# The first shift and scale of a decoder block, moved from VectorE to TensorE, with six projection blocks in step

## The chip, the cores and the metric

The kernel runs on one core of a Trainium2 chip. The metric is the device time of one execution, in microseconds (us). Five engines work side by side, each with its own list of instructions that it takes in order: TensorE (PE; its weight loads are shown apart, as PEld), VectorE (DVE), ScalarE (ACT), GpSimd (POOL) and SyncE (SP), which issues the DMA transfers. They wait for one another through semaphores.

## The reference, cut to what matters

A decoder block for one sequence of 2048 positions and 1024 channels, all in float32. A condition vector `c` gives six vectors of 1024 numbers, two of which, a shift and a scale, go into the first norm:

```python
cond = jax.nn.silu(c)
mod = (cond @ w_ada + b_ada)                 # 1024 x 6144
sh1, sc1, g1, sh2, sc2, g2 = split(mod, 6)
h = rms_norm(x, norm1_g) * (1 + sc1) + sh1
proj = h @ w_in                              # 1024 x 3088
# gated linear attention on 4 heads, dilated attention on 8 heads, one output projection
x = x + g1 * (mixed @ w_out)
# second norm with sh2, sc2; up projection, convolution of width 3, SwiGLU, down projection
x = x + g2 * ffn
```

Nothing of the projection can start before the shift and the scale are there for at least one group of 128 channels, and they need two sixths of `w_ada`, 8 MB.

## The kernel before, in words

The 2048 positions are four chunks of 512. Channels lie on the 128 partitions, so that 1024 channels are eight groups `k` = 0 to 7. A product in float32 is made of three faster ones (`mm3`, L234 to L241): the weight is split into a rounded part `whi` and the rest `wlo`, the activation into `hhi` and `hlo`, and three matmuls add hi by hi, lo by hi and hi by lo. `wslot` (L213) loads a weight block, ScalarE casts it to `whi` (L223), and VectorE or GpSimd subtracts to get `wlo` (L224).

At the start (`run`, L878) x of chunk 0 is loaded, `norm_stats` sums its squares (one matmul with a matrix of 1/1024, L318), and then for each `k` a shift and a scale are made by `ada(b)`, where `b` numbers the 48 groups of 128 columns of `w_ada`, 0 to 7 the shift and 8 to 15 the scale: a transposed weight block of 128 x 1024 is loaded (L275), VectorE multiplies it with `cond`, which lies in all partitions, and sums along the row (L281), then reads the sum out, adds the bias (L282) and, for the scale, makes `G` (L286). In this text such a multiply-and-sum is called a product. With them `norm_mod1` gives `hhi` (L333, ScalarE) and `hlo` (L335, VectorE) of that `k`. Four blocks of the projection (`FIRST`, channel blocks 0 to 3, the q and k of the gated attention) accumulate in four PSUM banks as the `k` come in. The low halves of their weights are all made on GpSimd.

The other 32 products (`b` = 16 to 47, shift, scale and gates of later stages) run beside the projections of all four chunks. They share one buffer (tile `v4`, one of it), so a load can start only when the product before it has read the buffer. The first of these loads, the load of the constants and the loads of x for chunk 1 each wait for a gate (`after`), the product of `k` = 6. A scheduler that works with a cost model at build time sets the final order on every engine, from the order in which the code hands the operations out. In the projection of chunk 0 (`proj`, L339) the four blocks already summed are stored first (`glaqk`), and then come the token-major block `tok(0)` (matmuls of 272 columns, its weight being 128x1088) and the blocks of the dilated attention (`qk`). The same `tok(0)` opens the projection of chunk 1. Later, `L552` copies the first state of the gated attention into `sbd`, after the last of the 32 products.

## Time and profile before

| | |
|---|---|
| median of 3 runs | 2752.87 us (2747.39 to 2753.99) |
| profiled execution, its own time | 2751.32 us |
| its span | 2749.5 us |
| mean granted TensorE clock | 0.984 |
| TensorE busy | 2658.3 us, 97% |
| VectorE busy | 1890.0 us, 69% |
| ScalarE busy | 1275.4 us, 46% |
| GpSimd busy | 515.7 us, 19% |

In the profile's rows the first number is the start in us from the start of the span, the second the duration, then engine, line, operation, output <- inputs and shapes; `xN` counts instructions, and brackets hold idle time before, with what ended it. In a table by windows each engine has its busy time with a count; PEclk is the clock that the throttle granted TensorE, as a share of full speed.

### The profile page before, as it was taken

What the parts mean: (1) busy time and instruction counts of PE and PEld (TensorE: products, weight loads), DVE (VectorE), ACT (ScalarE), POOL (GpSimd) and SP (SyncE); (2) the same over time, 40 slices, a digit from 0 to 9 for tenths busy, and PEclk for the clock granted to TensorE, in tenths of its full rate; (3) what the DMA queues carried; (4) which work ended last, traced back from release to release, by engine and by line L of the source; (5) the groups of instructions that cost most, each with busy time, mean ns of one, the idle gap of its engine ahead of it and who ended that gap; (6) DMA issues with size and microseconds to landing.
All of it is one profiled execution on the core that took longest, in us unless ns stands there. A gap on an engine that the chain in (4) does not pass through costs nothing.

```text
span 2749.5 us, 48364 instructions
## 1 busy us (share of the span) xinstructions
PE 2658.3 (97%) x18920; PEld 2178.2 (79%) x18920; DVE 1890.0 (69%) x3740; ACT 1275.4 (46%) x2607; POOL 515.7 (19%) x324
## 2 busy tenths in 40 slices
PE   5988999999999999999999999999999999999999
PEld 3977898888878777777777777887877778788887
DVE  8778676545578676667987667679676666566655
ACT  3555556564645434453544444345444443343332
POOL 1334322212224111101321101023111000021110
PEclk9998999999999999999999999999999999999999
DMA  7877465445722433346444334553444325332222
GB/s 272 289 257 235 144 200 172 154 156 168 243 84 94 135 121 113 105 141 206 135 124 127 111 121 128 176 167 104 142 129 131 123 90 181 129 100 97 95 100 92
DMA packets 196230, 405.19 MB, mean 147 GB/s; under 512 B 19473, under 2 KB 78626, under 8 KB 194722
## 3 DMA queue, kind: packets, MB, share of 16 engines
q1 hardware_dynamic: 196002, 402.11, 45.0%
q8 instruction: 149, 2.44, 0.4%
q14 instruction: 79, 0.65, 0.1%
HBM read 339.12 MB, written 62.91 MB: 146 GB/s over the span
## 4 chain that ended last, share of the span: by engine, by line
PE 78%; DVE 8%; DMA 6%; ACT 4%; issue 3%; POOL 1%; SPq 0%; ACTq 0%; POOLq 0%; DVEq 0%
PE psg L239 22%; PE psg L241 22%; PE psg L240 22%; DMA wada<-in_w_ada_dram 3%; PE psa L725 3%; PE psa L630 3%; PE psa L751 3%; DMA sq<-in_xT_dram 1%; DVE wada L281 1%; DVE wlo L224 1%; PE psa L500 1%; DVE pt L520 1%; ACT big L640 1%; ACT whi L223 1%; PE psa L650 1%
## 5 line engine op out<-in xcount | busy, mean ns | idle before, releaser
L239 PE MATMUL psg<-hhi,whi 128*128 128x512 f32 x2040 | 813.2, 401 | 19.6 <-ACT hhi L333 9.2
L240 PE MATMUL psg<-hlo,whi 128*128 128x512 f32 x2040 | 808.9, 397 | 5.6 <-DVE hlo L335 4.1
L241 PE MATMUL psg<-hhi,wlo 128*128 128x512 f32 x2040 | 808.5, 398 | 4.9 <-DVE wlo L224 4.8
L223 ACT CAST whi<-wraw 128x1024 fp32r<-128x1024 f32 x391 | 409.0, 1050 | 531.9 <-PE psg L240 375.4
L224 DVE TENSOR_TENSOR wlo<-wraw,whi 128x1024 fp32r<-128x1024 f32 (+1 forms) x300 | 388.3, 1296 | 163.1 <-ACT whi L223 148.7
L224 POOL TENSOR_TENSOR wlo<-wraw,whi 128x1024 fp32r<-128x1024 f32 x91 | 225.6, 2480 | 1433.0 <-ACT whi L223 1231.3
L239 PEld LDWEIGHTS psg<-hhi,whi 128*128 128x128 f32 x2040 | 389.0, 191 | 111.9 <-ACT hhi L333 12.2
L241 PEld LDWEIGHTS psg<-hhi,wlo 128*128 128x128 f32 x2040 | 389.0, 191 | 93.6 <-DVE wlo L224 6.4
L240 PEld LDWEIGHTS psg<-hlo,whi 128*128 128x128 f32 x2040 | 389.3, 191 | 91.5 <-DVE hlo L335 6.3
L239 PE MATMUL psg<-ghi,whi 128*128 128x512 f32 x704 | 277.9, 395 | 0.0
L241 PE MATMUL psg<-ghi,wlo 128*128 128x512 f32 x704 | 275.6, 392 | 1.1 <-DVE wlo L224 1.1
L240 PE MATMUL psg<-glo,whi 128*128 128x512 f32 x704 | 275.9, 392 | 0.0
L870 DVE SCALAR_TENSOR_TENSOR x<-psg,mod,x 128x512 f32<-128x512 f32 x192 | 143.0, 749 | 143.0 <-PE psg L241 138.3
L239 PE MATMUL psg<-whi,hhi 128*128 128x256 f32 (+1 forms) x768 | 220.9, 289 | 3.7 <-ACT hhi L333 1.9
L241 PE MATMUL psg<-whi,hlo 128*128 128x256 f32 (+1 forms) x768 | 220.4, 289 | 3.7 <-DVE hlo L335 3.7
L240 PE MATMUL psg<-wlo,hhi 128*128 128x256 f32 (+1 forms) x768 | 220.0, 287 | 0.4 <-DVE wlo L224 0.4
L826 DVE SCALAR_TENSOR_TENSOR y<-psg,conv_w_sb,y 128x511 f32<-128x511 f32 x176 | 130.6, 743 | 84.4 <-ACT y L825 84.1
L239 PEld LDWEIGHTS psg<-ghi,whi 128*128 128x128 f32 x704 | 132.2, 188 | 30.1 <-issue 2.9
L241 PEld LDWEIGHTS psg<-ghi,wlo 128*128 128x128 f32 x704 | 132.2, 188 | 30.0 <-DVE wlo L224 1.6
L240 PEld LDWEIGHTS psg<-glo,whi 128*128 128x128 f32 x704 | 132.3, 188 | 28.2 <-issue 2.1
L239 PEld LDWEIGHTS psg<-whi,hhi 128*128 128x128 f32 x768 | 147.9, 193 | 7.4 <-issue 2.2
L241 PEld LDWEIGHTS psg<-whi,hlo 128*128 128x128 f32 x768 | 147.9, 193 | 5.4 <-DVE hlo L335 4.4
(195 smaller groups left out, 3746.1 us busy)
## 6 DMA issues: line engine op xcount, KB each, us to landing
wraw<-in_w_up_dram SPq DMA_DIRECT2D x176, 512.0 KB, 3.4
wraw<-in_w_down_dram SPq DMA_DIRECT2D x88, 512.0 KB, 3.4
wraw<-in_w_ch_dram SPq DMA_DIRECT2D x48, 512.0 KB, 4.1
wada<-in_w_ada_dram SPq DMA_DIRECT2D x40, 512.0 KB, 5.0
wraw<-in_w_tok_dram SPq DMA_DIRECT2D x40, 512.0 KB, 4.3
v<-v SPq DMA_DIRECT2D x68, 256.0 KB, 4.2
wraw<-in_w_out_dram SPq DMA_DIRECT2D x32, 512.0 KB, 4.4
sq<-in_xT_dram SPq DMA_DIRECT2D x48, 256.0 KB, 3.9
```

Source lines behind the costliest of these rows:

```text
L223: nc.scalar.copy(hi[:, :n], raw[:, :n])
L224: (nc.gpsimd if pool else nc.vector).tensor_tensor(lo[:, :n], raw[:, :n], hi[:, :n].bitcast(F32), op=ALU.subtract)
L239: nc.tensor.matmul(ps, wh, hh, start=first and k == 0, stop=False, skip_group_check=shared)
L240: nc.tensor.matmul(ps, wh, hl, start=False, stop=False, skip_group_check=shared)
L241: nc.tensor.matmul(ps, wl, hh, start=False, stop=k == n - 1, skip_group_check=shared)
L281: self.last = nc.vector.tensor_tensor_reduce(raw, raw, self.cond[:, i * n:(i + 1) * n], 0.5, m if i else 0.0, ALU.mult, ALU.add, m)
L500: nc.tensor.matmul(sp[j:j + w, n * w:(n + 1) * w], kh[R, k0:k0 + w], qh[R, q0:q0 + w], start=True, stop=True)
L630: nc.tensor.matmul(ps[hh][:, e * 256 + z:(e + 1) * 256], q[H[hh], (i + e) * P:(i + e + 1) * P], key(H[hh], i + e, z), start=True, stop=Tru ...
L725: nc.tensor.transpose(ps[:n, i * P:(i + 1) * P], part(S[hh], i), self.C("id"))
L751: nc.tensor.matmul(out, lhsT, rhs, start=first[hh], stop=False, skip_group_check=True)
L826: nc.vector.scalar_tensor_tensor(y[:, 1:], ps[:, :T - 1], self.cw[:, 1, b:b + 1], y[:, 1:], op0=ALU.mult, op1=ALU.add)
L870: nc.vector.scalar_tensor_tensor(x1, ps, self.mod[:, 40 + cb:41 + cb], x1, op0=ALU.mult, op1=ALU.add)
```

## The change

The first 2048 columns of `w_ada` are laid out anew on the host, as `w_ada1`: four groups `u` of two `k` each, a group being four loads of 512 KB. `ada_first(u)` multiplies them on TensorE. The stationary side is `cond` with the 128 channels of group `k` on the partitions, the same number repeated in 32 columns (`crep`), the moving side 512 columns of `w_ada1`; the eight matmuls of a group go in turn to four bands of 32 columns of the array, each with 32 partitions of one PSUM bank. ScalarE copies the bank to SBUF, four small matmuls with a column of 1/64 (`sel`) sum the bands and turn the result onto the partitions, and VectorE adds the bias for two `k` of shift and of scale in one instruction (L310) and makes `G1` (L311). The 16 products of the first stage and their bias adds are gone from VectorE; the other 32 stay.

`FIRST` has six blocks where it had four, the two more being the first two of the dilated attention, in two banks of the other PSUM pool; after each group the matmuls of all six blocks for its two `k` are handed out. The low halves of blocks 1, 3 and 5 are made on GpSimd, those of 0, 2 and 4 on VectorE. The gate is now the bias add of group `u` = 2. In chunk 0, `qk(0)` and `qk(1)`, which are now only stored, come ahead of `tok(0)`.

```diff
-GATE = 6
-FIRST = (0, 1, 2, 3)
+FIRST = (0, 1, 2, 3, 4, 5)
...
+        self.sel = self.const.tile([P, 1], F32, name="sel")
+        nc.vector.memset(self.sel, 1.0 / 64)
+        tc_ = self.const.tile([P, KD], F32, name="tcol")
+        nc.scalar.activation(tc_, cc, AF.Tanh, scale=0.5)
+        self.crep = self.const.tile([P, KD, 32], F32, name="crep")
+        rep = lambda t: t[:, :, None].to_broadcast([P, KD, 32])
+        nc.vector.scalar_tensor_tensor(self.crep, rep(tc_), 1.0, rep(cc), op0=ALU.add, op1=ALU.mult)
...
+    def ada_first(self, u):
+        nc = self.nc
+        ps = self.pa()
+        raws = []
+        for i in range(4):
+            raw = self.at.tile([P, 1024], F32, name="wada", tag="big", bufs=4)
+            nc.sync.dma_start(raw, self.A["w_ada1"][u, i])
+            raws.append(raw)
+        for k in range(KD):
+            j = k % 4
+            nc.tensor.matmul(ps[32 * j:32 * j + 32], self.crep[:, k], raws[k // 2][:, k % 2 * T:(k % 2 + 1) * T], start=k < 4, stop=k >= 4, skip_group_check=True)
+        t = self.tmp.tile([P, T], F32, name="sq", bufs=3)
+        nc.scalar.copy(t, ps)
+        pm = self.pa()
+        for i in range(4):
+            nc.tensor.matmul(pm[:, i:i + 1], t[:, i * P:(i + 1) * P], self.sel, start=True, stop=True, skip_group_check=True)
+        v = lambda t: t.rearrange("p (a k) -> p a k", a=2)
+        two = slice(2 * u, 2 * u + 2)
+        self.gate_ins = nc.vector.tensor_tensor(v(self.mod[:, 0:16])[:, :, two], v(pm[:, 0:4]), v(self.ba[:, 0:16])[:, :, two], op=ALU.add)
+        nc.vector.scalar_tensor_tensor(self.G1[:, two], self.mod[:, 8 + 2 * u:10 + 2 * u], 1.0, self.n1[:, two], op0=ALU.add, op1=ALU.mult)
...
-        h0, ws, done = [], {}, {b: self.pg() for b in FIRST}
-        for k in range(KD):
...
-            gs = [self.ada(KD + k, big), self.ada(k, pair)]
...
-            if k == GATE:
-                self.gate_ins = self.last
-            h0.append(self.norm_mod1(xs[k], k, rstd[0], self.G1, self.mod[:, 0:8]))
-        for b in FIRST:
-            for k in range(KD):
-                self.mm3(done[b], ws[b][k:k + 1], h0[k:k + 1], k == 0, True)
+        h0, ws, at, done = [], {}, {}, {b: self.pg() if b < 4 else self.pa() for b in FIRST}
+        for u in range(4):
+            self.ada_first(u)
+            for b in {0: (0, 1, 2), 1: (3, 4), 2: (5,)}.get(u, ()):
+                src = self.A["w_ch"][b]
+                if b < 5:
+                    ws[b] = self.wblock(src, KD, P, b % 2 == 1, slot(b))
+                else:
+                    ws[b] = []
+                    for i, part in enumerate(slot(b)):
+                        ws[b] += self.wblock(src[:, i * T:(i + 1) * T], 4, P, True, part)
+            if u == 2:
+                gate = self.gate_ins
+            for k in (2 * u, 2 * u + 1):
+                h0.append(self.norm_mod1(xs[k], k, rstd[0], self.G1, self.mod[:, 0:8]))
+            for b in ws:
+                for k in range(at.get(b, 0), 2 * u + 2):
+                    self.mm3(done[b], ws[b][k:k + 1], h0[k:k + 1], k == 0, True)
+                at[b] = 2 * u + 2
+        self.gate_ins = gate
         self.consts()
...
-            yield from chain(glaqk(0), glaqk(1), glaqk(2), glaqk(3), tok(0), qk(0), qk(1), tok(1), ...)
+            yield from chain(glaqk(0), glaqk(1), glaqk(2), glaqk(3), qk(0), qk(1), tok(0), tok(1), ...)
```

The scheduler puts the rest of the work elsewhere too. Three places count for the prediction. In the changed kernel the lines of `ada` are L284 (product) and L285 (bias add), that of the weight's low half is L223, that of `hlo` L360, and each product is the row with `wada,mod`; the row after it reads the sum.

The first place is VectorE where the 32 products begin. Before, its order there is this, with the last `hlo` of the first stage on top, and the two rows of 128x1088 that are the low half of the weight of `tok(0)`:

```order
L335 SCALAR_TENSOR_TENSOR hlo<-x,mod,hhi 128x512
L281 ISA wada,mod<-wada,cond 128x1024
L281 ISA mod 128x1
L282 TENSOR_TENSOR mod<-mod,b_ada_sb 128x1
L314 COPY rstd<-sq 128x512
L224 TENSOR_TENSOR wlo<-wraw,whi 128x1088
L281 ISA wada,mod<-wada,cond 128x1024
L281 ISA mod 128x1
```

In the changed kernel two products stand ahead of the last group's bias add (L310), and these rows follow after it:

```order
L360 SCALAR_TENSOR_TENSOR hlo<-x,mod,hhi 128x512
L285 TENSOR_TENSOR mod<-mod,b_ada_sb 128x1
L341 TENSOR_TENSOR rstd<-rstd,sq 128x512 x2
L284 ISA wada,mod<-wada,cond 128x1024
L284 ISA mod 128x1
L285 TENSOR_TENSOR mod<-mod,b_ada_sb 128x1
L341 TENSOR_TENSOR rstd<-rstd,sq 128x512 x2
L284 ISA wada,mod<-wada,cond 128x1024
L284 ISA mod 128x1
L223 TENSOR_TENSOR wlo<-wraw,whi 128x1088
```

One product stood ahead of the low half of `tok(0)`'s weight, and five do now: two ahead of the last bias add, the third between the last two `hlo`, and the two that are shown.

The second place is VectorE where the products end. Before, the last of them stands right ahead of the copies of the first state:

```order
L281 ISA wada,mod<-wada,cond 128x1024
L281 ISA mod 128x1
L509 COPY_PREDICATED kt<-masks_sb,psa 128x128
L524 TENSOR_TENSOR pt<-kt,pt 128x512
L509 COPY_PREDICATED kt<-masks_sb,psa 128x128
L282 TENSOR_TENSOR mod<-mod,b_ada_sb 128x1
L509 COPY_PREDICATED kt<-masks_sb,psa 128x128
L552 COPY sbd_485<-kt 32x2x2x32 x4
```

Now the last one stands 35 rows ahead of those copies, where the 27th of the 32 stood:

```order
L284 ISA wada,mod<-wada,cond 128x1024
L284 ISA mod 128x1
L223 TENSOR_TENSOR wlo<-wraw,whi 128x1024
L486 SCALAR_TENSOR_TENSOR stage<-psa,stage 128x512
L285 TENSOR_TENSOR mod<-mod,b_ada_sb 128x1
L549 TENSOR_TENSOR pt<-kt,pt 128x512
```

From about the 8th product on, the products stand in front of the same work as before with five more of them ahead of it: 22 of 32 stood ahead of the first scaled x of chunk 1 (L331, L356 now), and 27 do now, while the other work around them has kept its order. After the state copies the lists of all engines are those of before, apart from a few neighbours that changed places.

The third place is SyncE, where the loads of the first stage are issued. Now the small loads (masks, convolution weights, norm gains, gate weights) and `gB`, which is copied to 128 partitions, come between the first group's weights and the second group's:

```order
L298 DMA wada<-in_w_ada_dram 128x1024 x4
L216 DMA wraw<-in_w_ch_dram 128x1024 x2
L150 DMA masks_sb<-in_masks_dram 128x160
L150 DMA conv_w_sb<-in_conv_w_dram 128x132
L150 DMA conv_b_sb<-in_conv_b_dram 128x44
L150 DMA q_norm_g_sb<-in_q_norm_g_dram 128x1
L150 DMA k_norm_g_sb<-in_k_norm_g_dram 128x1
L186 DMA gw<-in_gla_w_gate_dram 16x256
L187 DMA gw<-in_gla_b_gate_dram 1x256
L190 DMA gB<-in_gla_norm_g_dram 128x4x128
L298 DMA wada<-in_w_ada_dram 128x1024 x4
```

Before, they came after the weights of the first five pairs, in two parts:

```order
L275 DMA wada<-in_w_ada_dram 128x512 x2
L151 DMA masks_sb<-in_masks_dram 128x160
L151 DMA conv_w_sb<-in_conv_w_dram 128x132
L151 DMA conv_b_sb<-in_conv_b_dram 128x44
L151 DMA q_norm_g_sb<-in_q_norm_g_dram 128x1
L151 DMA k_norm_g_sb<-in_k_norm_g_dram 128x1
L275 DMA wada<-in_w_ada_dram 128x1024
L187 DMA gw<-in_gla_w_gate_dram 16x256
L217 DMA wraw<-in_w_ch_dram 128x1024
```

So the small loads have moved ahead of three of the four groups of the first weights.

More of the change, by code (lines that the diff above doesn't have):

```diff
@@ L278, in ada @@
         yield
         m = self.mod[:, b:b + 1]
-        for i, raw in enumerate(raws):
-            self.last = nc.vector.tensor_tensor_reduce(raw, raw, self.cond[:, i * n:(i + 1) * n], 0.5, m if i else 0.0, ALU.mult, ALU.add, m)
+        nc.vector.tensor_tensor_reduce(raw, raw, self.cond, 0.5, 0.0, ALU.mult, ALU.add, m)
         nc.vector.tensor_tensor(m, m, self.ba[:, b:b + 1], op=ALU.add)
-        for j, G, g in ((1, self.G1, self.n1), (4, self.G2, self.n2)):
-            if b // KD == j:
-                k = b % KD
-                nc.vector.scalar_tensor_tensor(G[:, k:k + 1], m, 1.0, g[:, k:k + 1], op0=ALU.add, op1=ALU.mult)
+        if b // KD == 4:
+            k = b % KD
+            nc.vector.scalar_tensor_tensor(self.G2[:, k:k + 1], m, 1.0, self.n2[:, k:k + 1], op0=ALU.add, op1=ALU.mult)
@@ L440, in proj @@
         if done:
-            yield from chain(glaqk(0), glaqk(1), glaqk(2), glaqk(3), tok(0), qk(0), qk(1), tok(1), qk(2), qk(3), tok(4), qk(4), tok(5), qk(5), qk(6), tok(2), qk(7), tok(3))
+            yield from chain(glaqk(0), glaqk(1), glaqk(2), glaqk(3), qk(0), qk(1), tok(0), tok(1), qk(2), qk(3), tok(4), qk(4), tok(5), qk(5), qk(6), tok(2), qk(7), tok(3))
         else:
@@ L901, in run, with slot @@
[L901 to L903 removed]
+        h0, ws, at, done = [], {}, {}, {b: self.pg() if b < 4 else self.pa() for b in FIRST}
+        def slot(b):
+            if b < 3:
+                return None
+            if b < 5:
+                t = self.at.tile([P, 2048], F32R, name="w0", tag="kt", bufs=2)
+                return t[:, 0:1024], t[:, 1024:2048]
+            return [(self.gp.tile([P, T], F32R, name="whi", tag="ghi"), self.gp.tile([P, T], F32R, name="wlo", tag="glo")) for _ in range(2)]
```

31 lines of the change are left out of this document (10 added, 21 removed).

## Prediction

> **What bounds the kernel now.** I read the page first: sums by engine and the chain that ended last.
>
> ```profile
> PE 2658.3 (97%) x18920; PEld 2178.2 (79%) x18920; DVE 1890.0 (69%) x3740; ACT 1275.4 (46%) x2607; POOL 515.7 (19%) x324
> PE 78%; DVE 8%; DMA 6%; ACT 4%; issue 3%; POOL 1%; SPq 0%; ACTq 0%; POOLq 0%; DVEq 0%
> ```
>
> TensorE is busy 97% of the span, so a change can win only where it is not. Behind about 310 us the lists of all engines are the same before and after, so I ask one question: when does the stage that ends at the copies of the first state (L552) end now? It ends at 268.42 us before. Windows show where TensorE idles until then.
>
> ```profile
> core 0: us, PE busy (x) PEld busy (x) DVE busy (x) ACT busy (x) POOL busy (x), PEclk, DMA share, GB/s
> 0.00:10.00 10.00, 0.00 (x0) 0.00 (x0) 4.87 (x10) 6.50 (x9) 1.19 (x6) 1.00 0.74 257
> 10.00:20.00 10.00, 2.08 (x2) 0.50 (x2) 9.04 (x15) 4.24 (x6) 2.34 (x1) 1.00 1.03 404
> 20.00:30.00 10.00, 5.01 (x12) 2.79 (x12) 10.00 (x22) 2.28 (x3) 2.65 (x1) 1.00 0.94 325
> 30.00:40.00 10.00, 4.75 (x10) 2.65 (x10) 10.00 (x26) 2.38 (x3) 2.35 (x1) 0.64 0.57 200
> 40.00:50.00 10.00, 9.34 (x29) 7.47 (x30) 9.93 (x18) 1.66 (x2) 2.41 (x1) 0.68 0.66 233
> 62.40:194.80 132.40, 126.56 (x822) 115.31 (x822) 94.29 (x136) 71.11 (x108) 39.55 (x27) 0.99 0.83 282
> 231.90:268.40 36.50, 27.86 (x440) 22.91 (x439) 33.87 (x51) 20.34 (x38) 22.05 (x15) 0.86 0.69 222
> ```
>
> From 20 to 50 us VectorE is full (10.00, 10.00, 9.93), TensorE half busy at clocks of 0.64 and 0.68, and the DMA falls to 200 GB/s: the products bound the start. From 62.4 TensorE idles 5.8 us in 132.4; in the last window 8.6 of 36.5, with VectorE at 33.87. So both ends of the stage are VectorE's. What it does at the start, and what the 32 later products wait for:
>
> ```profile
> L281 DVE CUSTOM_DVE_ANT_0 wada<-wada,cond 128x1024 f32<-128x1024 f32 x8 | 14.0, 1744 | 0.6 <-DMA wada<-in_w_ada_dram 0.6
> L282 DVE TENSOR_TENSOR mod<-mod,b_ada_sb 128x1 f32<-128x1 f32 x16 | 4.6, 287 | 0.0
> L281 DVE CUSTOM_DVE_ANT_0 wada<-wada,cond,mod 128x512 f32<-128x512 f32 x5 | 3.7, 746 | 0.0
> L281 DVE CUSTOM_DVE_ANT_0 ring<-ring,cond 128x1024 f32<-128x1024 f32 x3 | 3.6, 1220 | 0.0
> L281 DVE CUSTOM_DVE_ANT_0 wada<-wada,cond 128x512 f32<-128x512 f32 x5 | 3.4, 682 | 0.0
> L281 DVE DVE_READ_ACCUMULATOR2_ANT mod<- 128x1 f32 x21 | 1.7, 79 | 0.0
> L286 DVE SCALAR_TENSOR_TENSOR G<-mod,norm_g_sb 128x1 f32<-128x1 f32 x8 | 1.2, 151 | 0.0
> DVE wada L281 <- DMA wada<-in_w_ada_dram: 24.5, 18, 2.2
> ```
>
> The first seven are groups from 12 to 57 us; the last is a wait from 57 to 270 us. The later products go through one buffer: product, issue, transfer, next product. In 18 of 32 cases VectorE stood waiting for that transfer, 24.5 us. That ring is what I follow, through these rows of VectorE, the last being the state copies:
>
> ```profile
> 46.39 1.21 DVE L281 CUSTOM_DVE_ANT_0 wada<-wada,cond 128x1024 f32<-128x1024 f32 x1
> 59.58 1.23 DVE L281 CUSTOM_DVE_ANT_0 wada<-wada,cond 128x1024 f32<-128x1024 f32 x1
> 131.04 1.23 DVE L281 CUSTOM_DVE_ANT_0 wada<-wada,cond 128x1024 f32<-128x1024 f32 x1 [1.68 <-DMA wada<-in_w_ada_dram]
> 135.63 1.52 DVE L281 CUSTOM_DVE_ANT_0 wada<-wada,cond 128x1024 f32<-128x1024 f32 x1 [0.76 <-DMA wada<-in_w_ada_dram]
> 155.71 1.22 DVE L281 CUSTOM_DVE_ANT_0 wada<-wada,cond 128x1024 f32<-128x1024 f32 x1 [1.13 <-DMA wada<-in_w_ada_dram]
> 172.83 1.23 DVE L281 CUSTOM_DVE_ANT_0 wada<-wada,cond 128x1024 f32<-128x1024 f32 x1 [1.56 <-DMA wada<-in_w_ada_dram]
> 191.48 1.23 DVE L281 CUSTOM_DVE_ANT_0 wada<-wada,cond 128x1024 f32<-128x1024 f32 x1 [2.11 <-DMA wada<-in_w_ada_dram]
> 230.93 1.23 DVE L281 CUSTOM_DVE_ANT_0 wada<-wada,cond 128x1024 f32<-128x1024 f32 x1 [1.25 <-DMA wada<-in_w_ada_dram]
> 268.42 1.14 DVE L552 COPY sbd<-kt 32x128 f32<-32x128 f32 x5
> 57.00:192.70 135.70, 28.79 (x44) 0.99 0.82 278
> ```
>
> The first is the product that opens the gate. The last row counts L281 alone: 44 instructions, two to a product, so 22 products from 59.58 to 191.48, 21 intervals of 6.28 us. From 155.71 to 172.83 lie three of 5.71 each, all but one ended by the transfer; 131.04 to 135.63 is among the shortest, 4.59.
>
> **The change part by part.** *Removed:* 14.0 + 3.7 + 3.6 + 3.4 + 1.7 + 4.6 + 1.2 = 32.2 us of VectorE in the first stage, all on the path while it is full. New there are three weights' low halves (about 1.3 us each) and the small L310 and L311 for each group.
>
> *What is late next: the loads.* Up to the last load of the first 8 MB the queue carries cond 0.5, x 2.1, `w_ada1` 8.4, six weight blocks 3.1, one of `tok(0)`'s weights 0.6 and small ones 0.4, together 15.1 MB. The first 10 us move 2.6; the other 12.5 MB take 31 us at the 404 GB/s of 10:20, 54 us at the 233 of 40:50. Four buffers hold one group, so a group waits for the matmuls of the one before it; I take a rate near that of 20:30 and put the last group at 49 us (bounds 45 and 55, not below 41).
>
> *Added on TensorE:* 32 band matmuls and 16 small ones. Nearest rows: the float32 matmul of 512 columns in the first stage, and four bands in another stage:
>
> ```profile
> 14.96 2.08 PE L318 MATMUL psa<-rstd,ones 128*128 128x512 f32 x2 [14.96 <-DVE rstd L316]
> 60.97 0.39 PE L240 MATMUL psg<-hlo,w 128*128 128x512 f32 x1
> 61.20 0.39 PE L241 MATMUL psg<-hhi,w 128*128 128x512 f32 x1
> 62.42 0.39 PE L239 MATMUL psg<-whi,hhi 128*128 128x272 f32 x1 [0.84 <-ACT stg L388]
> 194.84 0.39 PE L239 MATMUL psg<-whi,hhi 128*128 128x272 f32 x1 [1.94 <-ACT hhi L333]
> 2250.82 1.10 PE L744 MATMUL psa<-v,pt 128*32 128x64 f32 x64
> 2251.85 1.10 PE L725 MATMUL psa<-consts_sb,big 128*128 128x128 f32 x8
> 52.02 0.43 SPq L275 DMA_DIRECT2D wada<-in_w_ada_dram  x1
> ```
>
> L744 takes about 0.9 of its 1.03 us for 64 records of 64 columns, 14 ns each, so the bands run together; at that rate two records of 512 columns per matmul cost 0.22, a group of eight 1.8 us, all 32 7.1. One after another each costs up to the cold 2.08 of L318, 16.6 a group. I take 1.8, since L744 has the same bands, and keep the other end as a rival. The 16 small ones have one moving column each; I give them nothing beside that.
>
> The Trainium skill, "TensorEngine Tiling (Array Packing)", Key Properties, speaks against the change: a change of tiling mode drains the array. The trace agrees in kind: from L744's last record to L725 about 0.14 us is left over. Entering and leaving the bands four times would make 8 x 0.14 = 1.1 us, less than what I round.
>
> *Blocks 4 and 5 in step:* 2 x 8 x 3 = 48 matmuls move from the later stage into the first. The four blocks ended at 61.6 (the row at 61.20 with its 0.39), and with 48 more at 0.227 us apart (the starts at 60.97 and 61.20, full clock) the same work would have ended at 61.6 + 10.9 = 72.5. With the last group at 49 us, its bias add behind two products, the last `hlo` at 65.5 and the rest of the 36 matmuls of two `k`, I get 69: a gain of 3.5 us, the whole of what the first stage gives directly.
>
> *The ring starts earlier.* Before, the gate product ended at 47.6, the first load was issued at 52.02, its product ran at 59.58. Now the gate is group 2's bias add, at about 46 (38 if the loads run at 404 GB/s, 50 at 233); issue 1.5 later behind the constants and 6.1 to land put product 1 at 53.6, 6 us earlier.
>
> *But more stands behind it.* Five products now stand ahead of the low half of `tok(0)`'s weight, where one did: the fifth at 53.6 + 4 x 5.8 = 76.8, the low half 1.3 later, 78. TensorE, done at 69, has nothing else in its list: some 8 us idle, and the 3.5 gained turn into 78 - 73.3 = 4.7 lost (73.3 is 62.42 + 10.9). It has slack to spend: 126.56 - 10.9 = 115.7 us of work lead from there to the first matmul of chunk 1, which could start at 194. But 27 products stand ahead of that one where 22 did. At a pace p the 27th is at 53.6 + 26p. I take p = 5.8: the ring alone does 5.7 where it is what is waited for, and I add 0.1 since other loads stand in the same queue. That gives 204.4, and the first matmul 3.4 later (as 194.84 follows 191.48), at 207.8: 13 us late.
>
> *And less after it.* Between product 22 and product 27 before lie 39.45 us (191.48 to 230.93); the same work with the same five products now lies between 27 and 32: 243.9. From there to the state copies it was 268.42 - 232.2 = 36.2 us with five products and their adds:
>
> ```profile
> L281 DVE CUSTOM_DVE_ANT_0 wada<-wada,cond 128x1024 f32<-128x1024 f32 x6 | 9.1, 1513 | 1.5 <-DMA wada<-in_w_ada_dram 1.5
> L282 DVE TENSOR_TENSOR mod<-mod,b_ada_sb 128x1 f32<-128x1 f32 x6 | 4.1, 691 | 0.0
> ```
>
> Less the one at 230.93 (1.2) and its add (0.15) these are 7.9 + 4.0 = 11.9 us on a full VectorE. Without them 24.3; TensorE's 27.86, in part at half clock, is 24.0 at full clock. I take 26, between the two readings. So the copies come at 243.9 + 1.2 + 26 = 271.1, against 268.42: **+2.7 us**, on 2751.32 makes 2754.0. The profiled execution lies 1.55 under the median of the runs shown, so I leave it there.
>
> The sum moves 26 us for each us of pace, and one for one with product 1. The 32 us of VectorE that are saved come out as nearly nothing, because a ring of transfers takes the place of the engine.
>
> **The rivals.** A measurement of this kernel tells about 0.3% from no change, 8.3 us.
>
> *The ring runs faster (faster).* With VectorE emptier, each product could run as its data land, at some 5.2 us, between the 4.59 and the 5.71. Then the fifth is at 74.4, product 27 at 188.8, chunk 1 starts at 192.2, 2.6 early, and the end gains 10.2 more: 2738. At 4.6 TensorE's own work bounds: `tok(0)` at 73, chunk 1 at 188.7, 6.1 early, 2735. It counts from a pace under 5.38. For it: the short rows; against: none of the three in a row between 155 and 173 came under 5.6.
>
> *The ring runs as it did (slower).* The place is the same buffer; at the old mean of 6.28 product 27 comes at 216.9, the state copies at 283.6, 15 us late: 2766. It decides from a pace of 6.02. For it: the DMA share is 0.83 there already, and other work on VectorE stretched the mean; against: five more products in the same work leave smaller lumps between them.
>
> *The bands don't run together (slower).* The change then doesn't do what it says: 8 x 2.08 = 16.6 us for a cold group in place of 1.8, 14.8 more, or 7.4 at full clock. The loads of the next group hide it for all but one of the groups that the gate waits for, so product 1 moves by 7 to 15 us and the end with it: 2761 to 2769, about 2765. Against it: L744.
>
> The Trainium skill, "TensorE: Matmul & The Clock Gate", Part 1, says that idle time of about 3.4 us throttles the array to half speed. The clocks of 0.64 and 0.68 above agree in kind. By it the 8 us of idle time ahead of `tok(0)` would cost a few us of cold matmuls, which the wait for product 27 takes up.
>
> **How the numbers follow.** Forecast (pace 5.38 to 6.02): 0.47, 2754. Faster ring 0.25. Old pace 0.22. Bands apart 0.06. So faster 0.25, same 0.47, slower 0.28. The likeliest one's own range is 2743 to 2763 (0.3% to both sides of before). The range of 8 in 10 takes in the faster ring down to 2736 and the old pace up to 2768; some 0.07 below and 0.12 above are left out.
>
> **What would show it.** Product 1 near 53.6; TensorE idle for some 8 us ahead of the first 272-column matmul, near 78; L298's groups landing from about 20 to 49 us; eight band matmuls (L302) in 2 to 4 us; VectorE's waits for `wada` up from 24.5 us towards 40; product 27 near 204, the 32nd near 244, the state copies near 271. I am wrong if the first matmul of chunk 1 starts under 200, if the lists behind the state copies don't run as before, or if the copies come before 260 or after 280.

## The result, and the profile after

| | before | after |
|---|---|---|
| median | 2750.52 us (4 runs, 2747.39 to 2753.99) | 2771.53 us (4 runs, 2765.69 to 2773.41) |
| ratio to before | | 1.0075, 95% interval 1.0062 to 1.0088 |
| profiled execution, its span | 2751.32, 2749.5 us | 2765.69, 2763.9 us |

The changed kernel is slower by 17 to 24 us. The forecast was no change, 2754, range 2736 to 2768: the time lies 3.5 us above it. The profiled execution is the fastest of the four, 14.4 us over that of before; what the other three lose beyond that has no profile.

The page of the changed kernel, engine sums and the chain that ended last. VectorE has lost 22 us, TensorE has gained 12.5.

```profile
PE 2670.8 (97%) x19016; PEld 2183.2 (79%) x19016; DVE 1868.0 (68%) x3685; ACT 1277.3 (46%) x2613; POOL 508.5 (18%) x324
PE 81%; DVE 7%; DMA 6%; ACT 4%; issue 2%; POOL 0%; SPq 0%; ACTq 0%; DVEq 0%; POOLq 0%
```

The windows from 10 to 50 us are those shown before the change. VectorE is no longer full there (1.72 us of work between 20 and 30), but the DMA falls to 120 GB/s between 20 and 30, TensorE does 1.05 us of work, and the stage goes on to 80 us and beyond.

```profile
core 0: us, PE busy (x) PEld busy (x) DVE busy (x) ACT busy (x) POOL busy (x), PEclk, DMA share, GB/s
10.00:20.00 10.00, 5.64 (x18) 1.22 (x18) 4.05 (x7) 5.10 (x9) 0.00 (x0) 1.00 0.98 378
20.00:30.00 10.00, 1.05 (x8) 0.97 (x8) 1.72 (x6) 1.38 (x2) 2.34 (x1) 0.69 0.42 120
30.00:40.00 10.00, 9.38 (x39) 4.05 (x39) 3.80 (x5) 3.97 (x5) 0.00 (x0) 0.79 0.88 342
40.00:50.00 10.00, 7.59 (x27) 5.81 (x27) 6.29 (x7) 3.02 (x5) 4.18 (x2) 0.83 0.58 199
70.00:80.00 10.00, 7.27 (x28) 5.00 (x27) 6.58 (x15) 3.76 (x6) 0.00 (x0) 0.75 0.56 172
88.00:218.00 130.00, 117.72 (x758) 107.95 (x759) 88.38 (x129) 64.39 (x98) 37.30 (x26) 0.95 0.81 267
```

VectorE in order of time: the four groups' bias adds (L310), the scaling of gB, which stands ahead of the first `G` (L311), then the first, 22nd, 27th and last product (L284), the first state copies (L577), and the first three scaled x of a later chunk (L356). The bias adds come 16 to 19 us apart; the first product runs at 66.62.

```profile
21.58 0.16 DVE L310 TENSOR_TENSOR mod<-psa,b_ada_sb 128x4 f32<-128x4 f32 x1 [0.77 <-PE psa L307]
29.21 0.43 DVE L191 TENSOR_SCALAR gB<-gB 128x512 f32<-128x512 f32 x1 [7.47 <-DMA gB<-in_gla_norm_g_dram]
29.55 0.15 DVE L311 SCALAR_TENSOR_TENSOR G<-mod,norm_g_sb 128x2 f32<-128x2 f32 x1
40.17 0.16 DVE L310 TENSOR_TENSOR mod<-psa,b_ada_sb 128x4 f32<-128x4 f32 x1 [2.23 <-PE psa L307]
40.37 2.08 DVE L311 SCALAR_TENSOR_TENSOR G<-mod,norm_g_sb 128x2 f32<-128x2 f32 x1
57.96 0.16 DVE L310 TENSOR_TENSOR mod<-psa,b_ada_sb 128x4 f32<-128x4 f32 x1 [10.80 <-PE psa L307]
66.62 1.23 DVE L284 CUSTOM_DVE_ANT_0 wada<-wada,cond 128x1024 f32<-128x1024 f32 x1 [0.90 <-DMA wada<-in_w_ada_dram]
74.24 0.16 DVE L310 TENSOR_TENSOR mod<-psa,b_ada_sb 128x4 f32<-128x4 f32 x1 [1.48 <-PE psa L307]
188.36 1.23 DVE L284 CUSTOM_DVE_ANT_0 wada<-wada,cond 128x1024 f32<-128x1024 f32 x1 [0.99 <-DMA wada<-in_w_ada_dram]
218.16 1.23 DVE L284 CUSTOM_DVE_ANT_0 wada<-wada,cond 128x1024 f32<-128x1024 f32 x1 [1.55 <-DMA wada<-in_w_ada_dram]
257.79 1.23 DVE L284 CUSTOM_DVE_ANT_0 wada<-wada,cond 128x1024 f32<-128x1024 f32 x1 [1.10 <-DMA wada<-in_w_ada_dram]
292.89 0.67 DVE L577 COPY sbd<-kt 32x128 f32<-32x128 f32 x3
314.31 2.08 DVE L356 SCALAR_TENSOR_TENSOR sq<-sq,G,rstd 128x512 f32<-128x512 f32 x3
```

The last row has its counterpart before, with which the loss is measured: the same three instructions, 18.75 us earlier.

```profile
295.56 2.08 DVE L331 SCALAR_TENSOR_TENSOR sq<-sq,G,rstd 128x512 f32<-128x512 f32 x3
```

At the state copies the lag is 24.5 us (292.89 against 268.42); by 314 it is 18.7, in the middle of the run about 18, and 14.4 at its end. So in the profiled execution the whole loss is made ahead of 300 us, as the prediction had it, and nothing behind that adds to it.

What TensorE and SyncE did in the first stage: the bands (L302; 16 records are a group), the block matmuls that follow an `hhi` (L238), the first matmul of 272 columns at 87.16; and on SyncE the last two small loads, the weights of group 1 (20.21), three pieces of block weights (39.28), the weights of group 3 (53.78) and the constants.

```profile
16.11 3.64 PE L302 MATMUL psa<-wada,crep 128*32 128x512 f32 x16
30.56 1.92 PE L302 MATMUL psa<-wada,crep 128*32 128x512 f32 x4 [9.02 <-DMA wada<-in_w_ada_dram]
44.04 1.41 PE L238 MATMUL psg<-hhi,whi 128*128 128x512 f32 x3 [2.41 <-ACT hhi L358]
52.69 1.92 PE L302 MATMUL psa<-wada,crep 128*32 128x512 f32 x16
87.16 0.28 PE L238 MATMUL psg<-whi,hhi 128*128 128x272 f32 x1
```

```profile
18.41 0.28 SPq L187 DMA_DIRECT2D gw<-in_gla_b_gate_dram  x1
19.71 0.40 SPq L190 DMA_DIRECT2D gB<-in_gla_norm_g_dram  x1
20.21 6.13 SPq L298 DMA_DIRECT2D wada<-in_w_ada_dram  x4
39.28 8.24 SPq L216 DMA_DIRECT2D wraw<-in_w_ch_dram  x3
53.78 1.75 SPq L298 DMA_DIRECT2D wada<-in_w_ada_dram  x4
58.15 0.33 SPq L174 DMA_DIRECT2D consts_sb<-in_consts_dram  x1
```

Group 1's weights are issued at 20.21, right behind the load of gB, and TensorE waits 9.02 us for them. What holds them is gB: its 256 KB, sent to 128 partitions, take 9.5 us from issue to landing, and the weights behind it land only after it. The kernel e9_gB_late issues the same weights at the same time with gB out of the way; there the first bands of group 1 run 7 us earlier, and the DMA moves 349 GB/s between 20 and 30 us instead of 120. The row of gB from the DMA view of 0 to 60 us of the changed kernel, and three of e9_gB_late:

```profile
gB<-in_gla_norm_g_dram SPq DMA_DIRECT2D x1, 256.0 KB, 9.5
```

```profile
20.11 1.77 SPq L300 DMA_DIRECT2D wada<-in_w_ada_dram  x4
23.53 1.92 PE L304 MATMUL psa<-wada,crep 128*32 128x512 f32 x4 [2.15 <-DMA wada<-in_w_ada_dram]
20.00:30.00 10.00, 7.52 (x24) 3.20 (x25) 6.36 (x9) 3.65 (x5) 2.34 (x1) 0.66 0.89 349
```

Group 2's bands stand behind the block matmuls of group 1 and run at 52.69. Only then are the four buffers free, and group 3's weights are issued at 53.78; the load of the constants waits for group 2's bias add until 58.15, and the ring behind it.

### The profile page after: what moved, and what is told of

It reads as the page before. It is cut to its first block, busy times and chain, and to the rows that moved or that the text cites. A ratio compares the mean times of both kernels' runs of the same rounds, so it can differ in the third digit from the quotient of the medians.

```text
span 2763.9 us, 48515 instructions
## 1 busy us (share of the span) xinstructions
PE 2670.8 (97%) x19016; PEld 2183.2 (79%) x19016; DVE 1868.0 (68%) x3685; ACT 1277.3 (46%) x2613; POOL 508.5 (18%) x324
## 4 chain that ended last, share of the span: by engine, by line
PE 81%; DVE 7%; DMA 6%; ACT 4%; issue 2%; POOL 0%; SPq 0%; ACTq 0%; DVEq 0%; POOLq 0%
PE psg L238 23%; PE psg L240 22%; PE psg L239 22%; DMA wada<-in_w_ada_dram 3%; PE psa L750 3%; PE psa L776 3%; PE psa L655 3%; DMA sq<-in_xT_dram 1%; PE psa L525 1%; ACT big L665 1%; DVE wlo L223 1%; DVE pt L545 1%; PE psa L675 1%; DVE wada L284 1%; PE psa L769 1%
## 5 line engine op out<-in xcount | busy, mean ns | idle before, releaser
L238 PE MATMUL psg<-hhi,whi 128*128 128x512 f32 x2024 | 804.9, 400 | 15.8 <-ACT hhi L358 5.7
L240 PE MATMUL psg<-hhi,wlo 128*128 128x512 f32 x2024 | 798.3, 395 | 4.8 <-DVE wlo L223 4.7
L239 PE MATMUL psg<-hlo,whi 128*128 128x512 f32 x2024 | 797.6, 394 | 0.0
L223 DVE TENSOR_TENSOR wlo<-wraw,whi 128x1024 fp32r<-128x1024 f32 (+1 forms) x300 | 387.6, 1294 | 166.0 <-ACT whi L222 152.3
L223 POOL TENSOR_TENSOR wlo<-wraw,whi 128x1024 fp32r<-128x1024 f32 (+1 forms) x91 | 224.3, 2464 | 1423.7 <-ACT whi L222 1310.8
L238 PEld LDWEIGHTS psg<-hhi,whi 128*128 128x128 f32 x2024 | 384.2, 190 | 107.4 <-ACT whi L222 9.0
L238 PE MATMUL psg<-ghi,whi 128*128 128x512 f32 x704 | 277.8, 395 | 0.0
L238 PE MATMUL psg<-whi,hhi 128*128 128x256 f32 (+1 forms) x768 | 223.0, 292 | 2.5 <-ACT hhi L358 1.4
L238 PEld LDWEIGHTS psg<-ghi,whi 128*128 128x128 f32 x704 | 132.2, 188 | 30.3 <-issue 2.9
L238 PEld LDWEIGHTS psg<-whi,hhi 128*128 128x128 f32 x768 | 149.6, 195 | 5.6 <-issue 2.0
```

The costliest lines, as they stand in the source:

```text
L223: (nc.gpsimd if pool else nc.vector).tensor_tensor(lo[:, :n], raw[:, :n], hi[:, :n].bitcast(F32), op=ALU.subtract)
L238: nc.tensor.matmul(ps, wh, hh, start=first and k == 0, stop=False, skip_group_check=shared)
L239: nc.tensor.matmul(ps, wh, hl, start=False, stop=False, skip_group_check=shared)
L240: nc.tensor.matmul(ps, wl, hh, start=False, stop=k == n - 1, skip_group_check=shared)
```

## The experiments

All times are medians, ratios go to the kernel before on the same chip, with 95% intervals. "Offset" is how late the same VectorE instructions run between 320 and 400 us against the profile of before, the median of that stretch; "chunk 1" the first scaled x of chunk 1 (L331, L356), 193.29 before.

| kernel | bias adds of groups 0 to 3 | product 1 | first 272-column matmul | chunk 1 | offset | us | ratio |
|---|---|---|---|---|---|---|---|
| before | | 59.6 | 62.4 | 193.3 | 0 | 2750.5 | 1 |
| changed | 21.6, 40.2, 58.0, 74.2 | 66.6 | 87.2 | 220.0 | 18.9 | 2771.5 | 1.0075 |
| e1_small_late | 21.9, 35.6, 55.6, 78.8 | 72.6 | 92.3 | 222.1 | 23.3 | 2770.6 | 1.0068 (1.0043 to 1.0092) |
| e2_gate1 | 21.5, 39.9, 57.7, 75.0 | 48.2 | 87.5 | 216.0 | 16.8 | 2765.5 | 1.0050 (1.0032 to 1.0068) |
| e3_bands_first | 20.8, 40.6, 54.9, 67.9 | 61.2 | 80.8 | 211.2 | 9.9 | 2762.2 | 1.0046 (1.0031 to 1.0061) |
| e4_ring4 | 21.0, 40.6, 58.3, 74.6 | 67.1 | 88.7 | 205.2 | 9.6 | 2760.9 | 1.0032 (1.0022 to 1.0041) |
| e5_four | 20.4, 40.0, 54.5, 64.3 | 61.2 | 74.6 | 211.6 | 13.5 | 2761.0 | 1.0041 (1.0028 to 1.0054) |
| e6_prefetch_six | 20.6, 37.5, 58.1, 75.9 | 65.4 | 88.4 | 219.9 | 20.4 | 2770.3 | 1.0072 (1.0056 to 1.0089) |
| e7_prefetch_four | 20.7, 32.6, 42.1, 57.5 | 51.7 | 70.5 | 205.0 | 4.5 | 2756.8 | 1.0020 (1.0010 to 1.0030) |
| e8_prefetch_four_ring4 | 20.6, 32.6, 41.8, 56.7 | 50.8 | 66.1 | 186.8 | -7.9 | 2741.0 | 0.9968 (0.9956 to 0.9981) |
| e9_gB_late | 21.4, 33.9, 51.8, 68.1 | 59.6 | 85.6 | 219.7 | 18.8 | 2767.9 | 1.0061 (1.0044 to 1.0078) |
| b1_before_ring4 | | 58.6 | 61.0 | 189.9 | -4.4 | 2745.0 | 0.9981 (0.9971 to 0.9990) |
| y2_six_all | 21.6, 25.4, 41.1, 64.4 | 48.2 | 83.5 | 214.8 | 14.3 | 2763.5 | 1.0047 (1.0032 to 1.0062) |
| y6_four_all | 20.5, 25.7, 41.4, 45.3 | 51.8 | 63.8 | 195.4 | -1.8 | 2747.7 | 0.9993 (0.9984 to 1.0002) |
| y3_six_all_ring4 | 20.8, 25.1, 41.1, 63.9 | 48.1 | 76.1 | 194.6 | -2.8 | 2749.8 | 0.9998 (0.9989 to 1.0008) |
| y5_four_bands_ring4 | 21.2, 25.0, 41.8, 45.7 | 52.2 | 61.3 | 180.8 | -13.5 | 2736.5 | 0.9949 (0.9935 to 0.9964) |

With six blocks 10.9 us of block matmuls are done ahead of the first 272-column matmul that come later with four; that much is to be taken off their numbers there before they are compared with four. The intervals of e1_small_late, e2_gate1, e6_prefetch_six and e9_gB_late overlap with that of the changed kernel, so their times alone show no gain.

**e1_small_late.** The small loads wait for the gate.

```diff
-        self.mk = self.cload("masks", MASKS.shape, U32)
+        def late(name, shape, dt=F32):
+            t = self.const.tile(list(shape), dt, name=name + "_sb")
+            self.after(nc.sync.dma_start(t, A[name]))
+            return t
+        self.mk = late("masks", MASKS.shape, U32)
...
```

> The changed kernel, with the small loads (masks, convolution weights, norm gains, gate weights, gB) waiting for the gate as the constants do, so that they no longer stand ahead of group 1's weights on SyncE. Theory A (the first stage's loads come late, product 1 of the ring with them, and the ring hands its start on to the end one for one): group 1's first band matmul near 23 instead of 30.56, product 1 near 59 instead of 66.62, pace unchanged at 5.8, 7 to 9 us less than the changed kernel, about 2763. Theory B (the six blocks' own matmuls on TensorE are late, whatever the loads do): product 1 may move, the time stays within 3 us of 2771. Theory C (the products are too slow, whenever they begin): the same as B.

Group 1's bias add came 4.6 us earlier, but product 1 came 6.0 later: the loads now stood between the constants and the ring's first load. The time did not move. The row of small loads does hold group 1, but mostly through gB: e9_gB_late, which moves gB alone, has nearly the whole gain there. Putting the loads in front of the ring only moves the wait. Theory A's forecast of product 1 near 59 failed through this edit's own side effect; the offset (4.4 more than the changed kernel) moved with product 1 (6.0 more).

**e2_gate1.** The gate one group earlier.

```diff
-            if u == 2:
+            if u == 1:
                 gate = self.gate_ins
```

> The changed kernel with the gate at group 1's bias add instead of group 2's: the ring, the constants and the loads of x for chunk 1 may start some 16 us earlier, and then share the DMA with the first stage's last groups. Theory A: product 1 near 50, product 27 near 202, from there TensorE's own work bounds (about 205): 12 to 16 us less, about 2757; less of it if the ring's loads push the last groups back. Theory B: no change, or a few us slower, since the last groups land later.

Product 1 came 18.4 us earlier, at 48.2, as A had it, but the 27th, at 212.9, only 5.3; the time fell 6 us and the offset 2.1. Most of the early start is gone by the second product: its load stood on SyncE behind group 3's weights and was issued at 55.33, so it ran at 63.39 (71.53 in the changed kernel). That is as early as in the kernel before (64.3), and still most of the loss stays. So a late start of the ring explains a small part of it; the token block still begins at 87.5, and five more products still stand ahead of chunk 1.

```profile
55.33 0.40 SPq L279 DMA_DIRECT2D wada<-in_w_ada_dram  x1
63.39 1.23 DVE L284 CUSTOM_DVE_ANT_0 wada<-wada,cond 128x1024 f32<-128x1024 f32 x1 [2.37 <-DMA wada<-in_w_ada_dram]
```

**e4_ring4.** Four buffers for the later products.

```diff
-        raw = self.at.tile([P, 1024], F32, name="wada", tag="v4", bufs=1)
+        raw = self.at.tile([P, 1024], F32, name="wada", tag="big", bufs=4)
```

> The changed kernel with the 32 later products in the four buffers of the first stage's weights instead of one buffer. If the ring of one buffer bounds the stretch from the first token block to chunk 1 (A and C): the mean interval falls from 5.8 to under 4.5, the first matmul of chunk 1 comes at about 205 (TensorE's own work) instead of 221, 10 to 16 us less, about 2758. Theory B: the products run earlier and the time stays within 3 us.

VectorE's waits for those loads went from 43.9 us to 3.0, the first scaled x of chunk 1 came 14.8 us earlier, at 205.2, and the time fell 10.6 us. (The 205 that was foretold was for the first matmul; its `hhi` began at 207.04.) The interval that was foretold doesn't apply: the scheduler now runs 19 products ahead of chunk 1, where it ran 27, and the other 13 from 228 us on, the last at 317. The same holds for the other kernels with four buffers (19 ahead of chunk 1, and 22 in the kernel before). So this edit takes waits and whole products from ahead of chunk 1, and no run holds the two apart. With the ring gone, 9.6 us of lateness stay. The waits of VectorE from 57 to 295 us, of the changed kernel and of this one:

```profile
DVE wada L284 <- DMA wada<-in_w_ada_dram: 43.9, 23, 5.1
```

```profile
DVE wada L284 <- DMA wada<-in_w_ada_dram: 3.0, 5, 1.1
```

**e5_four.** The bands alone, four blocks.

```diff
-FIRST = (0, 1, 2, 3, 4, 5)
+FIRST = (0, 1, 2, 3)
...
-            yield from chain(glaqk(0), glaqk(1), glaqk(2), glaqk(3), qk(0), qk(1), tok(0), tok(1), ...)
+            yield from chain(glaqk(0), glaqk(1), glaqk(2), glaqk(3), tok(0), qk(0), qk(1), tok(1), ...)
```

> The bands alone: four blocks in step and the order of chunk 0 as in the kernel before, everything else as changed. Theory A: the loads are late all the same (small loads still ahead), product 1 between 60 and 65, about 2765, still slower than before. Theory B (the two more blocks put 48 matmuls ahead of the last bands): product 1 near 54, the time at or under the kernel before, about 2750.

About halfway, 2761.0, with product 1 at 61.2: nearer to A than to B, and still slower than before. The two blocks cost some 10 us and the bands as they are built the other 10. Group 1 is as late as with six.

**e6_prefetch_six and e7_prefetch_four.** Groups 1 and 3 in other buffers.

```diff
         for i in range(4):
-            raw = self.at.tile([P, 1024], F32, name="wada", tag="big", bufs=4)
-            nc.sync.dma_start(raw, self.A["w_ada1"][u, i])
-            raws.append(raw)
+            if u % 2:
+                for j, tag in enumerate(("ghi", "glo")):
+                    raw = self.gp.tile([P, T], F32, name="wada", tag=tag)
+                    nc.sync.dma_start(raw, self.A["w_ada1"][u, i][:, j * T:(j + 1) * T])
+                    raws.append(raw)
+            else:
...
```

> The changed kernel, with groups 1 and 3 of the first weights in eight other buffers of half the size, so that a group's loads no longer wait for the matmuls of the group before it. Theory D (one group fills all the buffers; load, bands and block matmuls take turns, 16 to 18 us a group): groups' bias adds at about 21, 32, 44 and 55 instead of 22, 40, 58 and 74; first 272-column matmul near 72 instead of 87; 12 to 18 us less than the changed kernel, about 2756. Theory E (the bands stand behind the block matmuls on TensorE and come late whatever the loads do): bias adds move by under 4 us, time by under 4.

> Four blocks in step, the order of chunk 0 as before the change, and the eight more buffers. Theory D: bias adds at about 20, 30, 40 and 50, the first 272-column matmul near 58 (62.42 in the kernel before, 74.6 with four buffers), product 1 near 52, time about 2745, 4 to 6 us less than the kernel before. Theory E: near 2760, as with four buffers.

With six blocks the buffers brought nothing, which speaks against theory D as the whole cause. The profile shows where the gain went: gB, now queued behind more weights, held VectorE 11.20 us ahead of group 1's bias add; the blocks' weights issued behind gB from 27.14 on landed late, so that ScalarE's next cast ran at 40.89; and SyncE took 23.73 us over five pieces of them, ahead of the last group's.

```profile
37.12 0.43 DVE L191 TENSOR_SCALAR gB<-gB 128x512 f32<-128x512 f32 x1 [11.20 <-DMA gB<-in_gla_norm_g_dram]
37.46 0.16 DVE L316 TENSOR_TENSOR mod<-psa,b_ada_sb 128x4 f32<-128x4 f32 x1
```

```profile
27.14 23.73 SPq L216 DMA_DIRECT2D wraw<-in_w_ch_dram  x5
```

With four blocks the same buffers did act: groups 1 and 2 at 32.6 and 42.1 instead of 40.0 and 54.5, 4.2 us less in all, not the 16 that was foretold. The last group came at 57.5 (64.3 with four buffers, 50 foretold), and the time stayed over that of before.

**e3_bands_first.** The bands handed out ahead of the block matmuls of the group before.

```diff
+        self.ada_first(0)
         for u in range(4):
-            self.ada_first(u)
+            if u == 2:
+                gate = self.gate_ins
+            if u < 3:
+                self.ada_first(u + 1)
...
```

> The changed kernel with each group's bands handed out ahead of the block matmuls of the group before, buffers as they are. Theory E: groups 2 and 3 come 5 to 8 us earlier each, the first 272-column matmul near 77, about 2761. Theory D: the bands wait for their loads ahead of the block matmuls and hold these up in turn, since the buffers are the same four: bias adds within 4 us, time between 2766 and 2776.

Groups 2 and 3 came 3.1 and 6.3 us earlier, the token block 6.4, the time fell 9.3 to 2762.2: theory E, though group 2 gained less than foretold, and with no more buffers at all. The place of the bands in TensorE's list is a cause by itself.

**e9_gB_late.** The load of gB behind group 3's bias add.

```diff
+        gate, self.gate_ins = self.gate_ins, self.last_mod
-        nc.sync.dma_start(self.gB, ...)
+        self.after(nc.sync.dma_start(self.gB, ...))
+        self.gate_ins = gate
```

> The changed kernel with the load of gB alone put behind group 3's bias add, so that its scaling on VectorE no longer stands ahead of G of group 0, which waited 7.5 us for it. Theory G (that wait shifts the whole first stage): first h of group 0 at 24 instead of 30.5, groups' bias adds 5 to 7 us earlier, the first 272-column matmul near 81, about 2764. Theory D (buffers, then TensorE's order, set the pace): only group 0 moves, group 1's bands still start near 29 when their weights land, time within 3 us of 2771.

Half of each theory. The bias adds came 6 us earlier each, as G said, but both theories left out that gB had held group 1's weights in the DMA as well: with gB late its first bands ran at 23.53, not near 29. The time fell only 3.6 us, within the intervals, and the offset not at all, since TensorE then waited for a PSUM bank, to be stored by ScalarE, ahead of the token block:

```profile
85.60 0.59 PE L240 MATMUL psg<-whi,hhi 128*128 128x272 f32 x1 [5.72 <-ACT stg L415]
```

**e8_prefetch_four_ring4 and b1_before_ring4.** The ring's edit of e4_ring4 on the four-block kernel with more buffers, and on the kernel before.

> The kernel of e7_prefetch_four with the 32 later products in four buffers as in e4_ring4. If early start and ring both count, their gains add: the first matmul of chunk 1 near 180 (194.84 before), about 2738. If the ring only counts where the start is late, it is within 3 us of e7_prefetch_four.

> The kernel before, with the 32 later products in four buffers. If the ring bounds there too: chunk 1's first matmul near 188 instead of 194.84, 5 to 8 us less, about 2744. If it only bounds where the first stage is late: within 3 us of 2750.

The first fell by 15.7 us to 2741.0 and beats the kernel before; the second by 5.6 to 2745.0. The edit is worth something before the change too, but less.

**y2_six_all, y6_four_all, y3_six_all_ring4, y5_four_bands_ring4.** More buffers, bands ahead and gB late together, with six or four blocks and with one or four buffers for the later products; the edits are those above.

> Six blocks, with the three cures together: eight more weight buffers, the bands ahead of the block matmuls, gB late; one buffer for the later products as in the change. If these three are the whole lateness of the first stage: bias adds near 20, 31, 40 and 55, the first 272-column matmul near 73 (as the same work would have it in the kernel before), time 2750 to 2756. If the six blocks' weights hold the stage by themselves, group 3 stays beyond 65 and the time beyond 2760.

> The kernel of y2_six_all with four blocks in step and the order of chunk 0 as before the change: all three cures, one buffer for the later products. Theory S (the two more blocks hold the stage by themselves, through their weights, their 48 matmuls ahead of the last bands and the PSUM banks they keep): group 3's bias add near 46 instead of 64, the first 272-column matmul near 62 instead of 83.5, that is 10 us more than the 48 matmuls' 10.9, and 2748 against 2763.5. If the blocks only shift work: within 3 us of 2763.5.

> The kernel of y2_six_all with four buffers for the later products. Theory S: 10 us over the four-block kernel with the same cures (2736.5), about 2747. If six blocks lose only through the ring: within 3 us of 2736.5.

> The kernel of e8_prefetch_four_ring4, with the bands ahead of the block matmuls and gB late. If what is left of lateness there is group 3's bands (45.2 to 52 us, one piece at a time behind block matmuls): group 3's bias add at 48 instead of 56.7, the first 272-column matmul near 60 instead of 66, about 2736. If not, within 3 us of 2741.

| us | ring of one buffer | of four |
|---|---|---|
| six blocks | 2763.5 | 2749.8 |
| four blocks | 2747.7 | 2736.5 |

The two causes nearly add: the blocks, with the order of chunk 0 that goes with them, cost 15.8 and 13.3 us, the ring 13.7 and 11.2. Theory S holds in both columns; the four-block kernel with all cures and four buffers is 14 us faster than the kernel before, the best of the study. One caution on the corner of six blocks and one buffer: gB, put late, stood there ahead of the last group's `hlo` for 5.5 us, so some of its 2763.5 is gB's.

Why do blocks cost time that only move? The profiles show two things, and no run holds them apart. With six, the scheduler puts the last group's bands behind some 50 block matmuls; with four they run ahead of them (their bias add comes at 64 us with six and at 45 with four). The bands of group 3 in y3_six_all_ring4 and in y5_four_bands_ring4:

```profile
57.29 1.92 PE L310 MATMUL psa<-wada,crep 128*32 128x512 f32 x16
```

```profile
41.68 1.92 PE L310 MATMUL psa<-wada,crep 128*32 128x512 f32 x16
```

And the matmuls that were moved are missing later. Behind the first 272-column matmul, TensorE with six blocks is idle for 8.5 of 24 us, 6.2 of them on a copy of the gate's columns from the token block (`gl`), while VectorE is nearly full; with four it has the two blocks' matmuls to do there and never stops. The window and the wait of y3_six_all_ring4, then the window of y5_four_bands_ring4:

```profile
76.00:100.00 24.00, 15.48 (x110) 14.40 (x109) 21.78 (x37) 15.54 (x29) 7.95 (x4) 0.86 0.92 351
PE psa L482 <- ACT gl L451: 6.2, 1, 6.2
```

```profile
61.00:100.00 39.00, 39.00 (x261) 35.53 (x260) 30.34 (x56) 21.58 (x39) 3.90 (x3) 1.00 0.98 377
```

## Why the prediction was wrong

- **That the change acts ahead of 300 us alone, and that the saved 32 us of VectorE are not won:** right. The lag is 18.75 us at the rows of 295.56 and 314.31, and does not grow behind them.
- **"A group waits for the matmuls of the one before it; I take a rate near that of 20:30 and put the last group at 49 us (bounds 45 and 55, not below 41)":** this is the step that failed. It was a sum of bytes over a rate. The last weights were only issued at 53.78, and their bias add ran at 74.24. A rate says nothing of weights that land behind gB (group 1), of bands that stand behind some 40 block matmuls (group 2), and of loads that wait for buffers which those bands free (group 3). gB was in the sum as part of 0.4 MB of small loads, some 2 us at the lower rate; it took 9.5 us by itself (9.3 in the profile of before), about 7 of them on group 1's path. The order of the loads, and the four buffers, were before the prediction; the place of the bands was not asked for. e9_gB_late shows gB apart, e3_bands_first the place of the bands, and e7_prefetch_four, with four blocks, the buffers.
- **The gate "at about 46 (38 ..., 50 ...)", product 1 at 53.6:** the constants' load, which waits for the gate, went out at 58.15, and product 1 ran at 66.62. That is the same error passed on, 13.0 us.
- **"TensorE, done at 69, has nothing else in its list: some 8 us idle":** didn't happen. TensorE's own block work ran on to 87.16, and the low half behind the fifth product ran at 87.72; the idle time there is 1.6 us. The prediction had TensorE waiting for VectorE, and both were late.
- **The pace of 5.8:** right. From 66.62 to 188.36 it is 5.80, from 66.62 to 218.16 (26 intervals) 5.83, so product 27 lies 13.8 us behind the forecast of 204.4, of which 13.0 are the start. VectorE waited 43.9 us for the transfers; "towards 40" was foretold.
- **The same 39.45 us from product 27 to the last:** right, 257.79 - 218.16 = 39.63.
- **The last stretch, 26 us:** 292.89 - 258.94 = 34, so 8 us too little, but the lag fell by 5.8 us right behind it (24.5 to 18.7). The state copies were a bad place to close the sum.
- **The sum:** +2.7 by its own working, plus 13.0 for product 1 gives 15.7 us; the profiled execution has 14.4, the medians 21.0. That agreement is partly luck: the sum let the ring alone decide, and e2_gate1 shows that with the ring back at its old place from the second product on most of the loss stays. TensorE's token block was late as well (87.16 - 10.9 = 76.3, against 62.42).
- **The bands run together:** right, the rival falls; 16 records took 1.92 us at full clock, close to the 1.8 foretold. But a group ran in up to three pieces and partly cold:

```profile
L302 PE MATMUL psa<-wada,crep 128*32 128x512 f32 x64 | 13.0, 754 | 9.0 <-DMA wada<-in_w_ada_dram 9.0
L307 PE MATMUL psa<-sel,sq 128*128 128x1 f32 x32 | 4.1, 249 | 1.5 <-ACT sq L304 1.5
```

  13.0 us in place of 7.1, and the small matmuls, to which I gave nothing, 4.1. Together 17.1 against 7.1, with TensorE 97% busy.
- **"A gain of 3.5 us" from six blocks in step:** wrong in sign. They cost 10.5 us by e5_four, and 13 to 16 in the four corners. The prediction counted the matmuls as moved, and never asked what they had covered where they were.
- **The rivals:** the slower one that I gave 0.22 put the price on the pace, which didn't change; its 2766 was near for the wrong reason. A late first stage was only in the one with 0.06, which had it from bands that don't run together; late loads and bands late in TensorE's order were in none. Of the prediction's own signs of being wrong one came true: the state copies came after 280, at 292.89.
- **Two slips in its sums, without effect on the outcome:** the pace bound of 6.02 gives 2760 as the upper end of the likeliest range, not 2763; and bands one after another at full clock would cost 8.3 - 1.8 = 6.5 us more, not 7.4.

## What to carry to other kernels

When loads, their consumers and block work share buffers and in-order queues, work out the start of each group from its chain of issue, landing, matmul and free buffer, link by link through the listed order; bytes over a rate are only a floor, and a load takes what its own row shows (gB, 0.26 MB, 9.5 us). Where work is moved to an earlier stage, ask what it covered where it was. And where an engine is relieved, look at once for the single buffer behind which it then waits: here four buffers, with the new order of the products that came with them, were worth 11 to 16 us in the kernels with the bands, and 5.6 in the kernel before.

## What the runs showed of the hardware

One load of 256 KB can hold the queue for as long as several of 512 KB: gB, the same 512 bytes sent 4 times to each of 128 partitions, took 9.5 us from issue to landing, and from 20 to 28 us the DMA's share was 0.29 and its rate 56 GB/s, though four loads of 512 KB stood behind it; from 30 to 38 us, with gB landed, they were 0.99 and 393.

A GpSimd subtraction on 128x1024 held up even a very small VectorE instruction beside it: `G` for two columns took 2.08 us at 40.37, while this ran, and 0.15 at 29.55.

```profile
40.05 2.38 POOL L223 TENSOR_TENSOR w<-wraw,w 128x1024 fp32r<-128x1024 f32 x1 [16.26 <-ACT w L222]
```

The Trainium skill, "GPSIMD Engine Reference", section 1, Specifications, says that GpSimd's SBUF interfaces are shared with VectorE, with contention for instructions with two SBUF inputs. The trace agrees: `G` has two, and the loss is nearly the length of the subtraction. That an instruction on two columns pays as much as one on a thousand, the runs add: before the change, a product of 128x1024 at 16.96 took 3.27 us beside such a subtraction, and 1.22 at 13.07 without one.

From 11.4 to 20.2 us the small loads were issued up to 1.3 us apart, as 18.41 and 19.71 above show, though the first of these two is 1 KB. SyncE was waiting for earlier transfers to land: its waits from 11 to 20.5 us are two on x, four on `wada` and two on `wraw`, in the order of the loads that it had issued ahead of the small ones. So in this kernel a load of 1 KB waits its turn behind one of 0.5 MB, which takes 1.3 to 1.4 us at the 378 GB/s of that window. For group 1 this cost little: without the small loads its first weights were issued at 18.39 (e1_small_late), when the bands of group 0 had freed the first buffer, instead of 20.21.

```profile
SPq L150 <- DMA wada<-in_w_ada_dram: 2.8, 3, 0.9
```

The Trainium skill, "TensorEngine Tiling (Array Packing)", Key Properties, says that a change of tiling mode drains the array. The trace allows a small price at most: around the group at 52.69 the step into the bands is 0.32 us (52.37 to 52.69) and that of the first matmul behind them 0.34 (54.54 to 54.88), where 0.23 is steady, some 0.2 us a visit, and the groups made eight. That the drain is what costs this is not shown: in the kernel before, the step behind a mere wait, with no change of mode, is 0.34 too (59.48 to 59.82).

```profile
52.37 0.39 PE L239 MATMUL psa<-hlo,w 128*128 128x512 f32 x1
54.54 0.50 PE L240 MATMUL psa<-hhi,w 128*128 128x512 f32 x1
54.88 0.40 PE L238 MATMUL psa<-hhi,w 128*128 128x512 f32 x1
```
